# Two gate pairs a layer as plain filler units, a cover unit before the pairs, and the rotary tables built in the dense stage

## The chip, the core and the metric

The kernel runs on one core of a Trainium2 chip. The metric is the device time in microseconds (us) of one execution. Of the core's engines this text calls TensorE PE, VectorE DVE, ScalarE ACT, GpSimd POOL, and SyncE, which issues most of the DMA transfers, SP.

## What is computed

Two layers of a decoder trunk, 1024 tokens by 1024 channels in float32. From the normed input one product with `w_in` gives all that the three token mixers need, and the gates `g`:

```python
for l in range(DEPTH):
    h = rms_norm(x, norm_pre[l])
    u = h @ w_in[l]
    (a_q, a_k, a_v, a_z, b_q, b_kv, b_kr, b_z,
     c_q, c_k, c_v, c_z, g) = jnp.split(u, split_points, axis=-1)
    ...
    oa = diff_attention(..., lam, rel_bias)
    ob = mla_attention(q_nope, q_rope, k_nope, k_rope, v_m)
    oc = sliding_window_attention(..., sw_sinks[l], rel_bias)
    gates = jax.nn.sigmoid(g).reshape(B, S, N_BRANCHES, D_MODEL)
    y = (gates[:, :, 0] * ((oa * jax.nn.silu(a_z)) @ w_br_a[l])
         + gates[:, :, 1] * ((ob * jax.nn.silu(b_z)) @ w_br_b[l])
         + gates[:, :, 2] * ((oc * jax.nn.silu(c_z)) @ w_br_c[l]))
    x = x + rms_norm(y @ w_out[l], norm_post[l])
    x = x + jax.nn.sigmoid(x @ w_ple_gate[l]) * (p[l] @ w_ple_proj[l])
```

`lam` comes from four learned vectors a layer; the rotary part of the latent attention (MLA) needs the cosine and sine of position times frequency. The 3072 gate columns are 24 tiles of 128, eight for each branch, and are wanted only in the merge.

## The kernel before

**Products.** A float32 operand is split into a high and a low part, and a product is three matmuls (`group`, L296): high by high, high by low, low by high. A *unit* is one tile of 128 columns of `w_in` times the whole normed input: two halves of 512 tokens, eight blocks of 128 channels, three matmuls each, so 48 matmuls. It is a generator that yields after every six matmuls, and its weights come by `load_w` (L280): a DMA into one of two raw buffers (`wr`), a cast on ACT for the high part (L78), a subtraction on DVE or POOL (L93) for the low one; `le` says which. The matmuls of units carry the line L305, the split has L78 and L93 wherever it is used.

**A layer** runs these stages in order: an entry; `seven`, the dense stage; the sliding-window mixer `sw` (branch c); the differential mixer `da` (branch a); the latent entry `mla_entry` and the latent mixer `mla` (branch b); `merge`; and the tail with the output and embedding products.

**The dense stage** starts with the four z units of branch a, while DVE forms tiles `T`, sums and differences of blocks of the input. Then come *pairs*: `pair` makes two tiles of 128 columns with seven products in place of eight (Strassen's scheme over 2 x 2 blocks). Each product is 12 matmuls (L544), a pair 84. Its weights are two raw tiles, its combinations of weights `S` (L529), `aH` and `aL`; the sums of products `po` are made on DVE (L568, L583 and after). Four pairs are the z tiles of branches b and c (with silu on POOL), four are the gate tiles of branch a.

**Fillers.** The 16 gate tiles of branches b and c are plain units (`g_unit`), queued in `later` and taken out by `fill` and `weave` six matmuls at a time between the steps of a mixer. While gate units head the queue, each step adds `RATE` of the running mixer to a credit, and a chunk is taken when the credit reaches 1. A unit that is not used up by the mixers runs in full ahead of the merge. Its evictions are copied by ACT to `zs` (L78) and stored by SP to `g_d`. The merge loads the gates back, and applies the sigmoid to those of branches b and c.

**What is built once.** `setup_vecs`, `setup_lambda` and `setup_trig` run in layer 0's `sw`, between the two key groups. `setup_lambda` loads `lm` for each layer into one buffer (L180), POOL multiplies (L185), DVE sums (L187), ACT takes the exponent (L188). `setup_trig` computes the angles by some 40 operations of 128 x 128 on DVE, two sines on ACT (L252, L255), transposes on PE (L263), and stores the tables to `rope_d` for the latent entry.

**The latent entry** loads 416 columns of `w_in` in four chunks through the raw buffers `wr` (L1053), splits them into `WH` and `WL`, and makes eight row groups of 24 matmuls (stationary the input, moving 416 columns). `da` ends with a norm: ones products (L840), a square root on ACT (L896), reciprocal and product on DVE (L898); its result is transposed on PE (L639), which the program asks for behind the first row group.

**The order.** A scheduler places the instructions of each engine by priority and by what it believes to be ready; split and evictions are marked urgent (`high_priority`). Each engine then runs its own list in order. So where a filler stands is settled before the run.

Of the kernel before, what the change touches and what calls it, by code (L numbers as in the profile page):

```python
# [10 lines left out]
F32 = mybir.dt.float32  # L11
# [6 lines left out]
P = 128  # L18
S = 1024
D = 1024  # L20
DEPTH = 2
KT = D // P
# [6 lines left out]

RATE = dict(c=1.0, a=0.35, b=0.35)  # L30
BANKS = dict(mm=2, av=1, sc=3, tr=2)
# [29 lines left out]
class Builder:  # L61
# [44 lines left out]
    def setup(self):  # L106
# [3 lines left out]
        self.big = self.pool("big")  # L110
        self.w = self.pool("w")
        self.ent = ExitStack()
        pe = self.pool("entry", self.ent)
# [100 lines left out]

    def setup_trig(self, tp):
        nc, pi = self.nc, self.pi
        ang, v, k, d1, d0, a1 = (tp.tile([P, P], F32, name=n) for n in
                                 ("ang", "vv", "kk", "d1", "d0", "a1"))
        V = nc.vector
# [29 lines left out]
        V.tensor_scalar(ang, ang, PI_BELOW, -PI_BELOW, ALU.min, ALU.max)  # L249
        tr = tp.tile([P, 3, P], F32, name="trig")  # L250
        sn = tp.tile([P, 2, P], F32, name="sincos")
        nc.scalar.activation(sn[:, 0], ang, AF.Sin)  # L252
# [3 lines left out]
        V.tensor_scalar(tr[:, 0], sn[:, 0], -MLA_SCALE, None, ALU.mult)  # L256
        V.tensor_scalar(tr[:, 1:3], sn, MLA_SCALE, None, ALU.mult)

        self.cosT = self.cp.tile([P, 8, 2, 16], F32, name="cosT")
# [185 lines left out]

    def g_unit(self, l, bi, j):
        W = self.load_w(self.win(l, OFF["g"] + bi * D + j * P), le="g")

        def evac(hf, ps):
            st = self.zp.tile([P, 512], F32, tag="zs", bufs=2, name=self.uid("zs"))  # L450
            self.copy("a", st, ps)
            r0 = bi * D + j * P
            self.nc.sync.dma_start(self.g_d[r0:r0 + P, hf * 512:(hf + 1) * 512], st)

        yield from self.unit(W, KT, self.hT, evac)

    def seven(self, l):
        nc = self.nc  # L460
        with ExitStack() as ctx:
            z = [self.z_unit(l, "a", j) for j in range(4)]
            self.by_halves(*z[0:2])
            self.drain(*z[2:4])
            pl = self.pool("seven", ctx)
# [37 lines left out]
            for b in "bc":  # L503
                for j in (0, 2):
                    self.drain(self.pair(l, pl, T, OFF[b + "z"] + j * P, self.z_d[l, b], j * P, True))
            for j in range(0, KT, 2):
                self.drain(self.pair(l, pl, T, OFF["g"] + j * P, self.g_d, j * P, False))
# [149 lines left out]
    def sw(self, l):  # L657
        nc = self.nc
        with ExitStack() as ctx:
            pl = self.pool("sw", ctx)  # L660
# [26 lines left out]
            for g in range(2):  # L687
                if g == 1:
                    self.drain(*rest)
                    if not l:  # L690
                        self.setup_vecs()
                        self.setup_lambda(pl)
                        self.setup_trig(pl)
                for i in range(8):
# [348 lines left out]
    def mla_entry(self, l, p2, kH, kL, cq, ckv):  # L1043
# [13 lines left out]
        for hf in range(2):  # L1057
            raws = []
            st = p2.tile([P, 2, 4], F32, tag="st", bufs=2, name=self.uid("st"))
            for t in range(4):  # L1060
# [3 lines left out]
                                      lambda kt: tuple(x[:, sl] for x in self.hT[hf][kt]),  # L1064
                                      lambda kt: (WH[:, kt], WL[:, kt])), 1, not hf and t < 2)
                if self.rows_due:
# [67 lines left out]
    def merge(self, l):  # L1134
        nc, io = self.nc, self.io
        with ExitStack() as ctx:
# [50 lines left out]
            for bi, b in enumerate("abc"):  # L1187
                if b == "c":
                    self.yT = self.big_tiles()
                for j in range(KT):  # L1190
                    r0 = bi * D + j * P
                    s = pl.tile([P, S], F32, tag="sig", bufs=4, name=self.uid("sig"))
                    nc.sync.dma_start(s, self.g_d[r0:r0 + P, :])
                    if bi:
                        nc.scalar.activation(s, s, AF.Sigmoid)
# [160 lines left out]
    def build(self):  # L1356
# [3 lines left out]
        with self.ent:  # L1360
            self.entry()
            self.setup_bias(self.pe)
        self.zp = self.pool("zst")
        for l in range(DEPTH):
            self.seven(l)
            self.units = self.later(*[self.g_unit(l, bi, j) for bi in (1, 2) for j in range(KT)])
            for b, mixer in (("c", self.sw), ("a", self.da), ("b", self.mla)):
                self.rate = RATE[b]
                mixer(l)
            self.merge(l)  # L1370
            self.tail(l)
# [24 lines left out]
```

## Time and profile before

| | us |
|---|---|
| three runs | 2654.86 to 2656.57, median 2655.8 |
| the profiled execution | 2653.98 |
| its span in the trace | 2652.2 |

| engine | busy us | share of the span |
|---|---|---|
| PE | 2587.8 | 98% |
| DVE | 1659.6 | 63% |
| ACT | 1265.6 | 48% |
| POOL | 452.6 | 17% |

The busy time of PE counts matmuls; weight loads run beside them and are listed as PEld. A busy time is a sum over stages. Stages of the profiled execution, from the timeline (layer 0 and layer 1): z units 33 to 71 and 1342 to 1384; pairs to 229 and 1548; sliding window from 275 to 400 and from 1595 to 1700; differential mixer from 435 to 657 and from 1735 to 1974; latent entry to 738 and 2052; latent mixer to 937 and 2253; left-over gate units to 991 and 2305; then merge and tail. In a row of the timeline the figure in brackets is the engine's idle time ahead of the instruction, and behind the arrow stands what ended it.

### The profile page before, as it was taken

To read this page: it belongs to the slowest core of one execution; us is meant where nothing else is said; L and a number is where in the kernel's file an instruction comes from. 1 tells how busy PE (TensorE), PEld (TensorE's weight loads), DVE (VectorE), ACT (ScalarE), POOL (GpSimd) and SP (SyncE) were. 2 spreads that over 40 slices of the span, in tenths; PEclk is the share of its full clock that TensorE was granted. 3 is DMA by queue.
4 is the path that set the end of the run, shared out by engine and by line. 5 is a ranking of instruction groups with operands and counts; after the bars stand their busy time and mean duration, and the time that the engine had idled before them with its cause. 6 is when DMAs were issued, how large, how long until landed. Compare 5 with 4: busy or idle time off the path is not lost. (4 is left out here: it accounts for less than half of the span.)

```text
span 2652.2 us, 35930 instructions
## 1 busy us (share of the span) xinstructions
PE 2587.8 (98%) x12832; PEld 2120.4 (80%) x12832; DVE 1659.6 (63%) x3312; ACT 1265.6 (48%) x2761; POOL 452.6 (17%) x375
## 2 busy tenths in 40 slices
PE   8999999999999999999999999999999999999999
PEld 6778777888878878888877887888878788888887
DVE  7654565777378756755475536457764787577553
ACT  5433654555377733433443436545553777234332
POOL 2210000000010114234412001000000111251441
PEclk9999999999999999999999999999999999999999
DMA  6233123111110169453332331322111101894442
GB/s 197 86 116 109 46 69 104 53 52 48 51 31 23 53 210 290 148 177 115 116 96 90 114 99 50 94 68 60 51 53 40 29 22 54 267 280 148 137 118 96
DMA packets 296818, 269.21 MB, mean 102 GB/s; under 512 B 24272, under 2 KB 237456, under 8 KB 296512
## 3 DMA queue, kind: packets, MB, share of 16 engines
q1 hardware_dynamic: 295568, 262.19, 33.1%
q0 software_dynamic: 1072, 4.73, 0.6%
q8 instruction: 101, 1.65, 0.3%
q14 instruction: 77, 0.63, 0.1%
HBM read 194.93 MB, written 61.44 MB: 97 GB/s over the span
## 5 line engine op out<-in xcount | busy, mean ns | idle before, releaser
L305 PE MATMUL mm<-big,wH 128*128 128x512 f32 x3456 | 1106.5, 395 | 4.9 <-ACT zs L78 2.4
L305 PEld LDWEIGHTS mm<-big,wH 128*128 128x128 f32 x3456 | 638.9, 188 | 128.7 <-ACT zs L78 3.2
L305 PE MATMUL mm<-big,wL 128*128 128x512 f32 x1728 | 680.0, 394 | 2.3 <-POOL wL L93 1.9
L305 PEld LDWEIGHTS mm<-big,wL 128*128 128x128 f32 x1728 | 324.9, 188 | 65.7 <-POOL wL L93 2.8
L78 ACT CAST wH<-wr 128x1024 fp32r<-128x1024 f32 (+3 forms) x252 | 212.2, 852 | 334.4 <-PE mm L305 230.4
L93 DVE TENSOR_TENSOR wL<-wr,wH 128x1024 fp32r<-128x1024 f32 (+2 forms) x220 | 222.6, 1021 | 234.4 <-ACT wH L78 229.8
L793 ACT ACTIVATE e<-sc,st 128x512 f32<-128x512 f32 (+3 forms) x384 | 221.7, 582 | 99.5 <-DVE st L790 71.7
L787 DVE TENSOR_REDUCE st<-sc 128x1 f32<-128x512 f32 (+3 forms) x384 | 209.1, 551 | 7.2 <-PE sc L104 3.4
L93 POOL TENSOR_TENSOR wL<-wr,wH 128x1024 fp32r<-128x1024 f32 x32 | 77.4, 2423 | 501.7 <-ACT wH L78 336.6
L78 ACT CAST wtH<-tr 128x512 fp32r<-128x512 f32 x204 | 115.4, 590 | 82.5 <-PE tr L822 65.4
L93 DVE TENSOR_TENSOR wtL<-tr,wtH 128x512 fp32r<-128x512 f32 x204 | 136.3, 682 | 27.4 <-ACT wtH L78 26.9
L822 PE MATMUL tr<-cm,e 128*128 128x128 f32 x864 | 148.4, 275 | 1.0 <-DVE e L933 0.5
L544 PE MATMUL mm<-T,aH 128*128 128x512 f32 x384 | 121.5, 397 | 4.6 <-DVE po L583 3.9
L822 PEld LDWEIGHTS tr<-cm,e 128*128 128x128 f32 x864 | 106.1, 141 | 20.3 <-ACT e L793 7.0
L104 PE MATMUL sc<-kA,q 128*128 128x256 f32 (+3 forms) x320 | 104.6, 337 | 1.6 <-ACT e L735 0.8
L104 PE MATMUL sc<-kB,q 128*128 128x256 f32 (+3 forms) x320 | 99.6, 320 | 0.0
L544 PEld LDWEIGHTS mm<-T,aH 128*128 128x128 f32 x384 | 70.6, 188 | 26.3 <-DVE po L583 9.8
L544 PE MATMUL mm<-big,wH 128*128 128x512 f32 x256 | 82.9, 397 | 8.4 <-ACT po L78 8.4
L93 POOL TENSOR_TENSOR kL<-vT,kH 64x512 fp32r<-64x512 f32 x32 | 42.2, 1318 | 265.6 <-ACT kH L78 200.2
L379 POOL TENSOR_TENSOR acc<-acc,sq 128x512 f32<-128x512 f32 x36 | 56.8, 1577 | 176.2 <-ACT sq L378 176.2
L913 DVE TENSOR_TENSOR sc<-sc,dab 128x256 f32<-128x256 f32 (+1 forms) x128 | 52.4, 412 | 47.8 <-PE sc L104 46.6
L305 PE MATMUL mm<-WH,big 128*128 128x416 f32 x256 | 76.9, 370 | 3.6 <-ACT WH L78 2.7
(340 smaller groups left out, 5065.3 us busy)
## 6 DMA issues: line engine op xcount, KB each, us to landing
wr<-w_in SPq DMA_DIRECT2D x108, 512.0 KB, 3.8
sig<-g_d SPq DMA_DIRECT2D x48, 512.0 KB, 6.0
g_d<-zs SPq DMA_DIRECT2D x64, 256.0 KB, 2.2
wr<-w_out SPq DMA_DIRECT2D x32, 512.0 KB, 4.1
wr<-w_ple_gate SPq DMA_DIRECT2D x32, 512.0 KB, 4.0
kB<-kA SPq DMA_DIRECT2D x80, 128.0 KB, 2.3
x<-x SPq DMA_DIRECT2D x16, 512.0 KB, 6.1
g_d<-sg SPq DMA_DIRECT2D x32, 256.0 KB, 2.1
```

The lines of the kernel that those rows point to most:

```text
L78: nc.scalar.copy(out, in_)
L93: (nc.vector if le == "v" else nc.gpsimd).tensor_tensor(L, src, h, ALU.subtract)
L104: self.nc.tensor.matmul(ps, w, x, start=i == 0, stop=i == n - 1)
L305: self.nc.tensor.matmul(ps, w, x, start=i == 0, stop=i == n - 1)
L379: (nc.gpsimd if eng == "g" else nc.vector).tensor_tensor(st, st, sq, ALU.add)
L544: nc.tensor.matmul(ps, w, x, start=start and not i, stop=i == 11, skip_group_check=True)
L787: nc.vector.tensor_reduce(st[:, c:c + 1], ps[:, :w], AX.X, ALU.max, negate=len(ch) == 1)
L793: nc.scalar.activation(e[:, k0:k0 + w], pss[c][:, :w], AF.Exp, bias=st[:, 0:1], accum_out=sums[:, c:c + 1])
L822: self.nc.tensor.transpose(tr[:, (2 * a + q) * P:(2 * a + q + 1) * P], ws[q][:, kt * P:(kt + 1) * P], self.ident)
L913: nc.vector.tensor_tensor(ps[:, a - k0:w], ps[:, a - k0:w], bias[:, h, a - n + 256:k0 + w - n + 256], ALU.add)
```

## The change

- `PAIRED = 4`: only gate tiles 0 to 3 are still made by pairs (two pairs a layer). Tiles 4 to 7, which also belonged to pairs, join the units: 20 units a layer in place of 16. The merge applies the sigmoid to all tiles from 4 on.
- `RATE` rises from 0.35 to 0.4 in the differential mixer and to 0.45 in the latent one.
- In the latent entry all eight row groups are woven with a filler chunk after each six matmuls, at no credit; before, the first two of the first half were, and the others by credit.
- One unit, gate tile 23, is taken out of the queue and runs in the dense stage right behind the z units (the cover unit).
- `setup_trig` moves to the dense stage: its first part runs behind the pairs of branch b, its transposes and stores behind those of branch c. It works in three of the slots of the `T` tiles. `setup_vecs` and `setup_lambda` stay where they were.

```diff
-RATE = dict(c=1.0, a=0.35, b=0.35)
+RATE = dict(c=1.0, a=0.4, b=0.45)
+
+PAIRED = 4
...
-    def setup_trig(self, tp):
+    def setup_trig(self, room):
...
-        ang, v, k, d1, d0, a1 = (tp.tile([P, P], F32, name=n) for n in
-                                 ("ang", "vv", "kk", "d1", "d0", "a1"))
+        ang, v, k, d1, d0, a1 = (room[i // 4][:, i % 4 * P:i % 4 * P + P] for i in range(6))
...
         V.tensor_scalar(tr[:, 1:3], sn, MLA_SCALE, None, ALU.mult)
+        yield
...
-    def g_unit(self, l, bi, j):
-        W = self.load_w(self.win(l, OFF["g"] + bi * D + j * P), le="g")
+    def g_unit(self, l, n, le="g"):
+        bi, j = n // KT, n % KT
+        W = self.load_w(self.win(l, OFF["g"] + n * P), le=le)
...
             self.by_halves(*z[0:2])
-            self.drain(*z[2:4])
+            self.drain(*z[2:4], self.g_unit(l, 3 * KT - 1, le="v"))
...
-            for j in range(0, KT, 2):
+                if not l:
+                    if b == "b":
+
+                        trig = self.setup_trig([slot() for _ in range(3)])
+                    next(trig, None)
+            for j in range(0, PAIRED, 2):
                 self.drain(self.pair(l, pl, T, OFF["g"] + j * P, self.g_d, j * P, False))
...
                         self.setup_lambda(pl)
-                        self.setup_trig(pl)
...
-                                      lambda kt: (WH[:, kt], WL[:, kt])), 1, not hf and t < 2)
+                                      lambda kt: (WH[:, kt], WL[:, kt])), 1, True)
...
-                    if bi:
+                    if bi * KT + j >= PAIRED:
                         nc.scalar.activation(s, s, AF.Sigmoid)
...
-            self.units = self.later(*[self.g_unit(l, bi, j) for bi in (1, 2) for j in range(KT)])
+            self.units = self.later(*[self.g_unit(l, n) for n in range(PAIRED, 3 * KT - 1)])
```

How this moves instructions is shown at three places of PE's list. `mm` and `sc` are accumulators, `big` the parts of the normed input, `wH` and `wL` the split weights of a unit or of a pair's first tile. The lines of the changed kernel are a few higher (L305 is L309, L544 is L554, L639 is L649, L840 is L849).

Layer 0, PE, the end of the z units, before: the pair's first product follows the last z unit.

```order
L305 MATMUL mm_594<-big_164,wL_562 128x512
L305 MATMUL mm_594<-big_166,wH_561 128x512
L305 MATMUL mm_594<-big_167,wH_561 128x512
L305 MATMUL mm_594<-big_166,wL_562 128x512
L544 MATMUL mm_766<-big_136,wH_754 128x512
L544 MATMUL mm_766<-big_137,wH_754 128x512
```

The same place after: the last rows of the cover unit, which began 48 rows earlier, behind the last z unit.

```order
L309 MATMUL mm_657<-big_165,wL_626 128x512
L309 MATMUL mm_657<-big_167,wH_625 128x512
L309 MATMUL mm_657<-big_168,wH_625 128x512
L309 MATMUL mm_657<-big_167,wL_626 128x512
L309 MATMUL mm_657<-big_169,wH_625 128x512
L309 MATMUL mm_657<-big_170,wH_625 128x512
L309 MATMUL mm_657<-big_169,wL_626 128x512
L554 MATMUL mm_828<-big_139,wH_816 128x512
```

So 48 matmuls of a unit now stand between z units and pairs, in both layers.

Layer 0, PE, from the end of the differential mixer into the latent entry, before. `ms` is that mixer's norm, `WH` and `WL` the entry's weights; the six unit rows are the last of 17 behind the ones products.

```order
L305 MATMUL mm_6228<-big_164,wH_6175 128x512
L305 MATMUL mm_6228<-big_165,wH_6175 128x512
L305 MATMUL mm_6228<-big_164,wL_6176 128x512
L305 MATMUL mm_6228<-big_166,wH_6175 128x512
L305 MATMUL mm_6228<-big_167,wH_6175 128x512
L305 MATMUL mm_6228<-big_166,wL_6176 128x512
L639 MATMUL tr_6329<-cm,ms_3526 32x128
L305 MATMUL mm_6283<-WH_6264,big_136 128x416
L305 MATMUL mm_6283<-WL_6265,big_136 128x416
```

The same place after:

```order
L815 MATMUL av_5874<-wd_3283,VH_4908 128x256
L815 MATMUL av_5874<-wd_3282,VL_4909 128x256
L849 MATMUL av_5990<-ones,sq_5987 128x1 x2
L649 MATMUL tr_6125<-cm,ms_3291 32x128
L309 MATMUL mm_6069<-WH_6050,big_139 128x416
L309 MATMUL mm_6069<-WL_6051,big_139 128x416
L309 MATMUL mm_6069<-WH_6050,big_140 128x416
L309 MATMUL mm_6069<-WH_6050,big_141 128x416
```

No unit matmul is left between the ones products and the transpose of `ms`; the next one comes behind all 24 matmuls of the first row group.

Layer 1, PE, the same seam, before:

```order
L305 MATMUL mm_18387<-big_11772,wH_18334 128x512
L305 MATMUL mm_18387<-big_11771,wL_18335 128x512
L840 MATMUL av_18362<-ones,sq_18359 128x1 x2
L639 MATMUL tr_18488<-cm,ms_15685 32x128
L305 MATMUL mm_18442<-WH_18423,big_11741 128x416
L305 MATMUL mm_18503<-WH_18423,big_11741 128x416
```

And after, the end of the eleven unit rows that stand there now:

```order
L309 MATMUL mm_18146<-big_11709,wH_18142 128x512
L309 MATMUL mm_18146<-big_11708,wL_18143 128x512
L309 MATMUL mm_18146<-big_11710,wH_18142 128x512
L309 MATMUL mm_18146<-big_11711,wH_18142 128x512
L309 MATMUL mm_18146<-big_11710,wL_18143 128x512
L649 MATMUL tr_18247<-cm,ms_15410 32x128
L309 MATMUL mm_18201<-WH_18182,big_11696 128x416
```

In layer 1 the unit moved the other way: into the gap between the ones products and the transpose.

Over the whole program the unit matmuls of a layer go from 768 to 960. By stage, before and after, layer 0: dense stage 0 and 48, sliding window 192 and 158, differential mixer 192 and 226, latent entry 54 and 150, latent mixer 140 and 160, ahead of the merge 190 and 218. Layer 1: 0 and 48, 158 and 158, 226 and 250, 60 and 132, 134 and 163, 190 and 209.

## Rows read from the trace of the kernel before

**Rows 1.** The page's first part: busy us, share, instructions of each engine.

```profile
PE 2587.8 (98%) x12832; PEld 2120.4 (80%) x12832; DVE 1659.6 (63%) x3312; ACT 1265.6 (48%) x2761; POOL 452.6 (17%) x375
```

**Rows 2.** Busy time by stage: stretch, length, engines, granted clock, DMA share, GB/s.

```profile
275.40:400.00 124.60, 117.98 (x607) 96.40 (x605) 79.77 (x274) 74.31 (x217) 11.00 (x8) 0.97 0.24 60
...
657.50:738.00 80.50, 76.60 (x386) 66.18 (x386) 35.50 (x91) 28.08 (x71) 6.47 (x8) 0.98 0.15 46
738.00:937.00 199.00, 194.77 (x1177) 159.10 (x1176) 155.00 (x373) 147.79 (x397) 28.20 (x19) 1.00 0.13 36
...
1595.00:1700.00 105.00, 103.14 (x551) 83.67 (x550) 69.98 (x226) 69.49 (x211) 9.66 (x5) 1.00 0.23 64
...
1974.50:2052.00 77.50, 71.24 (x353) 61.48 (x353) 32.97 (x86) 25.14 (x66) 5.66 (x3) 0.96 0.16 46
```

**Rows 3.** Timeline of PE in a dense stretch of layer 1: start, us, instruction.

```profile
1358.28 0.62 PE L305 MATMUL mm<-big,wH 128*128 128x512 f32 x2
1358.73 0.39 PE L305 MATMUL mm<-big,wL 128*128 128x512 f32 x1
```

**Rows 4.** Busy time in three stretches: PE, PEld, DVE, ACT, POOL, clock.

```profile
33.00:71.00 38.00, 37.24 (x163) 30.16 (x162) 35.96 (x56) 16.70 (x27) 0.00 (x0) 1.00 0.34 103
110.00:130.00 20.00, 19.68 (x86) 15.84 (x85) 11.40 (x16) 7.77 (x12) 5.71 (x5) 1.00 0.34 106
343.00:356.40 13.40, 9.25 (x38) 7.45 (x37) 11.26 (x44) 4.18 (x7) 2.46 (x1) 0.85 0.27 82
```

**Rows 5.** Timeline of PE at the start of layer 1's first pair.

```profile
1397.02 1.22 PE L544 MATMUL mm<-big,wH 128*128 128x512 f32 x2 [7.47 <-ACT po L78]
...
1400.49 0.39 PE L544 MATMUL mm<-big,wL 128*128 128x512 f32 x1
```

**Rows 6.** Waits of PE from 30 to 110 us: total us, times, longest.

```profile
PE mm L544 <- DVE po L583: 1.6, 2, 1.3
PE mm L544 <- ACT po L78: 1.0, 1, 1.0
```

**Rows 7.** Timeline of PE in layer 0's sliding window.

```profile
353.45 0.47 PE L263 MATMUL tr<-cm,sincos 128*128 128x128 f32 x1 [4.15 <-ACT sincos L252]
```

**Rows 8.** Timeline of SP and POOL in layer 0's sliding window: the lambda chain.

```profile
333.45 0.58 SPq L180 DMA_DIRECT2D lm<-da_lambda  x1
...
337.61 0.46 POOL L185 TENSOR_TENSOR pr<-lm 128x128 f32<-128x128 f32 x1 [3.90 <-DMA lm<-da_lambda]
...
341.59 0.46 POOL L185 TENSOR_TENSOR pr<-lm 128x128 f32<-128x128 f32 x1 [3.52 <-DMA lm<-da_lambda]
```

**Rows 9.** Timeline of PE from layer 1's norm into its latent entry.

```profile
1984.66 0.37 PE L639 MATMUL tr<-cm,ms 128*32 128x128 f32 x1 [2.21 <-DVE ms L898]
1985.70 1.03 PE L305 MATMUL mm<-WH,big 128*128 128x416 f32 x2 [0.67 <-ACT WH L78]
...
1990.64 0.45 PE L305 MATMUL mm<-WL,big 128*128 128x416 f32 x1
...
1999.67 0.50 PE L305 MATMUL mm<-big,wL 128*128 128x512 f32 x1 [0.95 <-POOL wL L93]
```

**Rows 10.** Timeline of ACT, SP and PE at the start of layer 0's latent entry.

```profile
664.67 0.37 ACT L78 COPY o<-av 128x256 f32<-128x256 f32 x1 [1.55 <-PE av L806]
...
667.76 1.68 ACT L78 CAST WH<-wr 128x832 fp32r<-128x832 f32 x2 [0.77 <-DVE ms L898]
...
672.04 0.91 SPq L1053 DMA_DIRECT2D wr<-w_in  x2
...
675.75 0.89 ACT L78 CAST WH<-wr 128x832 fp32r<-128x832 f32 x1 [5.12 <-DMA wr<-w_in]
...
676.68 1.06 PE L305 MATMUL mm<-WH,big 128*128 128x416 f32 x2 [2.01 <-ACT WH L78]
...
677.72 1.43 SPq L277 DMA_DIRECT2D wr<-w_in  x2
...
681.63 1.05 ACT L78 CAST wH<-wr 128x1024 fp32r<-128x1024 f32 x1 [3.94 <-DMA wr<-w_in]
...
685.18 0.50 PE L305 MATMUL mm<-big,wL 128*128 128x512 f32 x1 [0.94 <-POOL wL L93]
```

More of the change, by code (lines that the diff above doesn't have):

```diff
@@ L111, in setup @@
         self.w = self.pool("w")
+        self.zp = self.pool("zst")
         self.ent = ExitStack()
@@ L249, in setup_trig @@
         V.tensor_scalar(ang, ang, PI_BELOW, -PI_BELOW, ALU.min, ALU.max)
-        tr = tp.tile([P, 3, P], F32, name="trig")
-        sn = tp.tile([P, 2, P], F32, name="sincos")
+        tr = room[2][:, 0:3 * P].rearrange("p (a j) -> p a j", j=P)
+        sn = room[1][:, 2 * P:4 * P].rearrange("p (a j) -> p a j", j=P)
         nc.scalar.activation(sn[:, 0], ang, AF.Sin)
@@ L1362, in build @@
             self.setup_bias(self.pe)
-        self.zp = self.pool("zst")
         for l in range(DEPTH):
             self.seven(l)
-            self.units = self.later(*[self.g_unit(l, bi, j) for bi in (1, 2) for j in range(KT)])
+            self.units = self.later(*[self.g_unit(l, n) for n in range(PAIRED, 3 * KT - 1)])
             for b, mixer in (("c", self.sw), ("a", self.da), ("b", self.mla)):
```

## The prediction

> **What bounds the kernel now.** I read the busy shares first. TensorE (PE) is busy 2587.8 us of 2652.2 [rows 1], so the end moves only if PE gets fewer matmuls, shorter waits, or less time at the lower clock. The windows by stage say where the waits are [rows 2]: the sliding-window mixer of layer 0 idles 6.62 us of 124.6, its twin in layer 1 1.86 of 105.0; the latent entries idle 3.90 and 6.26 us; the granted clock is under 1.00 in all of these but the twin. Then the order of the changed kernel shows, on PE, what stands in each hole, and I go back to the timeline for what each hole costs. All is counted against the profiled execution (2653.98 us); the median of the three runs is 2655.8, 1.8 higher, and I add the difference to the median.
>
> **More matmuls: +10.8 us.** Where nothing waits, two matmuls of 512 columns take 0.45 us from start to start, 0.225 each [rows 3]. A pair makes two tiles with seven products of 12, 84 matmuls; two plain units take 96. Two pairs in each of two layers become units: 4 x 12 = 48 more, 48 x 0.225 = 10.8, all on PE. The order counts the same: 960 gate-unit matmuls a layer where 768 stood. The waits of pairs that the profile names lie in the first ones and in those with silu, so I let nothing come back with the gate pairs. The Trainium skill ("TensorE: Matmul & The Clock Gate", Back-to-back issue gap) has a sustained 131 ns for 512 columns; by it this term would be 6.3 us. The rows here say 225, and the measurement decides.
>
> **Cover unit: -11.9 us (-8 to -13).** Between the last z unit and the first pair now stand 48 matmuls of a gate unit, 10.8 us, which need only the normed input. What they cover is the wait for VectorE, which forms the T tiles and is busy 35.96 us of 38 there [rows 4]. In layer 1 PE idles 7.47 us before the pair's third product and then runs eight matmuls from 1397.02 to 1400.49 at the lower clock, 3.47 us in place of 1.80 [rows 5]; the starts on either side of the hole make it 7.6, so 9.3 in all. The hole is under 10.8, so the unit covers it whole. In layer 0 the waits before the pairs' products are 1.6 + 1.0 us by cause [rows 6]. The unit's own split adds one VectorE pass of 1.2 us, and if its weights come late the gain shrinks: the low end, -8. The 48 matmuls are no cost here: they left the mixers.
>
> **Tables out of the mixer, layer 0: -5.3 us (-7.5 to +1).** In the mixer PE waits 4.15 us for the sine [rows 7], and then runs at the lower clock until 359; the stage as a whole idles 4.8 us more than its twin and grants 0.97 against 1.00 [rows 2]. From 353.45 to 359 at half rate 2.8 us are lost: together 7.6. After the change PE's order there is that of layer 1 but for two exchanges. What stays is the lambda chain: two loads one behind the other on SP through one buffer, then a GpSimd product, then VectorE. GpSimd waited 3.90 and 3.52 us for its loads [rows 8] and VectorE for GpSimd, and nobody minded, since some hundred unit matmuls, 23 us, ran. Those matmuls are gone from there. From the first load's issue (333.45) to the second product's end (341.59 + 0.46) are 8.6 us [rows 8]. VectorE's score reductions and ScalarE's exponents are queued behind. Laid over layer 1's timeline, the products come about 1 us after each is wanted: 2.2 us, nearer to the small end of 0.5 to 8.6, because two score tiles are already through. -7.5 + 2.2 = -5.3 (at 8.6, +1).
>
> **The tables in the dense stage: +1.0 us (0 to +12).** VectorE's table work is 11.3 us of 13.4 in the old place [rows 4]. It now lies in two pairs of 20 us, each with 11.4 us of VectorE work [rows 4]: 17 of 20 us, no overflow. But the pairs wait for VectorE's sums, in order; one sum late by some short operations of 0.28 us gives about 1 us. Eight stores of the tables precede one weight load on SP, which is wanted a pair later. ScalarE reloads its function tables three times more, with 12 us of 20 free [rows 4]. If nothing overlaps, all of the 11.3 us shows: the high end.
>
> **Latent entry of layer 1: -6.2 us (-3 to -9).** Before, PE reaches the norm chain (square root, reciprocal, transpose) with no unit matmul left: 2.21 us, 0.67 for a weight cast, then a run at the lower clock to 1990.64, 14 matmuls of 416 columns 0.353 us apart in place of 0.183 (0.225 x 416/512): 2.4; and a wait of 0.95 for GpSimd's weight split [rows 9]. Sum 6.2. In the new order 11 unit matmuls (2.5 us) stand in the norm chain, and the second half of that unit, its weights long loaded, follows.
>
> **Latent entry of layer 0: +8 us (+4 to +13).** Here it is the reverse. Before, 17 unit matmuls cover the norm chain; PE idles 2.01 us for the third weight chunk, runs slowly to 680 (about 2.3 by the same count), and waits 0.94 for GpSimd's split [rows 10]: 5.3. After, the unit ends before the last weighted block, the transpose of the norm follows the ones product at once, and all 24 products of the first row group stand in a row. The next unit's weights come fifth through two raw buffers, behind four chunks. Its hole in steps, from rows of before [rows 10]: the norm chain from the last product's eviction (664.67) to the first cast (667.76) and its 0.9: 3.5 us idle. The third chunk may be issued when the first chunk's split on VectorE ends, about 669.7 (the third one's cast ends at 676.64 and the load behind its split goes at 677.72, so a split is 1.1), and lands 3.7 later as it does now (672.04 to 675.75), cast 0.9: 674.3; PE has done its 12 products at 671, idle 3.3. The unit's load goes after the third chunk's split, at 675.4, lands 3.9 later (677.72 to 681.63) and is cast in 1.05: 680.3, where PE was done at 676.7: 3.6. Then 1.5 for the GpSimd split (2.4 us less the work beside it), and 1.6 to 2.3 at the lower clock. Sum 13.5 to 14.2, less 5.3: 8.2 to 8.9; I take 8, since the last weighted block may slip into the first hole.
>
> **The rest of both entries: -1.7 us (-3 to 0).** Of the idle time [rows 2] 2.4 us in layer 1 and 0.95 in layer 0 are short waits that I haven't named. The change weaves a chunk of unit matmuls after each chunk of all eight row groups (before: the first two), 96 and 72 matmuls more: half of it may go.
>
> **Mixers at the higher rate: -2 us (-4 to +3).** Layer 0's latent mixer idles 4.2 us of 199 [rows 2], in many short waits. 20 more unit matmuls there, and 29 in layer 1, may take a quarter of it in each, a us apiece; if they push the softmax's products later, it costs as much. For the differential mixer I take nothing. The merge's four more sigmoids a layer lie on a ScalarE that is a third busy: nothing.
>
> **Sum.** 10.8 - 11.9 - 5.3 + 1.0 - 6.2 + 8 - 1.7 - 2 = -7.3. Profiled 2646.7; on the median 2648.5.
>
> **The rivals.**
> *Both entries run full (faster still).* If the scheduler's order matters less than I think and the weights of layer 0's unit arrive with the chunks, the +8 falls to 0 or below, as in layer 1: 2640.5, and with no cost of lambda 2638.3. For it: the split is marked urgent. Against it: two raw buffers and an in-order SP. Chance 0.15.
> *Lambda's chain takes the place of the sine (no change).* If the chain lies bare for its 8.6 us in place of 2.2, the mixer gives back 6.4: 2654.9. For it: the 7.4 us that its loads took. Against it: score tiles ahead of it. Chance 0.22. The same time comes out if the fillers' extra matmuls in the mixers find no hole and the cover gives only its low end (2 and 3.9 gone: 2654.4).
> *The dry entry of layer 0 (slower).* If after each of its three holes PE stays at the lower clock until 690, the 24 chunk products (4.5 us) and some 30 of the unit (6.8) cost twice their time: 11.3 us, less the 2 already counted, 9 more. The unit's load behind the norm's row store on SP could add 3 to 4 more, and one more run at the lower clock 2. It decides from 20.5 us in this stretch, for which all of it must come: 2661 and more, to 2664. For it: after the holes of [rows 5] and [rows 9] the clock was low for 3.5 and 5 us. Against it: three separate runs would need 20 us of low clock, and no row shows such a run. Chance 0.15. The Trainium skill (the same page, Part 1) calls half rate the resting state that activity lifts; that speaks for this rival, and the trace agrees as far as each of the long holes is followed by such a run.
> *It does not do what it says.* Cover and fillers stand in the order, so only their weights could fail; that is the low end above.
>
> **How the numbers follow.** My forecast has 0.48 with its own range 2643 to 2654, the rivals 0.15, 0.22 and 0.15. A measurement of this kernel can tell about 0.2%, 5.3 us. Of the forecast's 0.48 some 0.13 lie above 2650.5, so faster is 0.35 + 0.15 and a little of the second rival: 0.52; same 0.13 and most of the 0.22, less what of both ends over 2661: 0.31; slower 0.15 and that: 0.17. The range is 2638 to 2663: the better case's lower end and the slower case's upper one lie outside with some 0.08 each.
>
> **What would show it.** Right: no PE wait over 1 us before layer 1's first pairs; 48 matmuls of a unit ahead of them; layer 0's mixer without the sine's wait, with one of 1 to 3 us for lambda; 13 to 14 us lost between the last weighted block and the first unit in layer 0's entry, and nearly none in layer 1's. Wrong: pairs three and four of layer 0 longer than 20.5 us (tables), lambda's wait over 5 us, or layer 0's entry as full as layer 1's.

## The result, and the profile after

The changed kernel takes 2668.62 us (four runs, 2666.64 to 2673.01) against 2655.33 before (the median of four): a ratio of 1.0051, with an interval of 1.0036 to 1.0066. It is slower by 13.3 us, where 2648.5 was forecast, and it lies above the range, which ended at 2663.

The page's first part of the kernel after, to be read against [rows 1]:

```profile
PE 2602.3 (98%) x12880; PEld 2132.9 (80%) x12880; DVE 1615.2 (61%) x3254; ACT 1261.1 (47%) x2747; POOL 465.8 (17%) x381
```

48 matmuls more, as counted; 14.5 us more of busy PE, of which 10.8 are theirs. The span is 2667.3 us, 15.1 longer.

To find the place I cut both executions into stretches at the same instructions (first and last product of the pairs, transposes of the mixers, first step of the merge), and took from each stretch its matmuls at the pace of full speed: 0.227 us for 512 columns, in proportion for fewer. What is left is time lost to waits, to the lower clock and to switches between operations. Its change, after less before:

| stretch | layer 0 | layer 1 | forecast, both |
|---|---|---|---|
| 48 more matmuls | +5.4 | +5.4 | +10.8 |
| z units to the last pair | -4.3 | -10.2 | -10.9 |
| sliding window, to the differential mixer | -5.9 | +1.5 | -5.3 |
| differential mixer | +1.2 | +0.7 | 0 |
| latent entry, with what leads to the latent mixer | +7.4 | -4.6 | +0.1 |
| latent mixer | -1.9 | +3.1 | -2 |
| left-over units ahead of the merge | **+6.4** | **+7.0** | 0 |
| merge, then tail | 0 | +4.0 | 0 |

The gains are there, and larger than forecast where they were largest. The loss stands in a row that the sum did not have: the left-over units between the last product of the latent mixer and the merge, 13.4 us. Busy time by stage of the kernel after (columns as in [rows 2]):

```profile
250.00:348.00 98.00, 94.93 (x512) 76.99 (x510) 66.72 (x214) 65.31 (x199) 10.95 (x8) 1.00 0.25 60
632.00:722.00 90.00, 83.42 (x369) 70.43 (x368) 24.28 (x63) 22.97 (x56) 10.47 (x5) 0.92 0.20 58
...
936.00:998.30 62.30, 57.92 (x246) 46.65 (x245) 25.91 (x32) 16.83 (x27) 12.29 (x7) 0.95 0.78 247
...
1957.00:2036.00 79.00, 75.94 (x360) 66.02 (x359) 22.08 (x62) 21.60 (x55) 8.12 (x4) 0.98 0.20 60
...
2256.40:2316.00 59.60, 55.89 (x239) 45.46 (x238) 23.82 (x32) 16.34 (x26) 12.78 (x7) 0.94 0.77 248
```

The same view of the kernel before, for the two stretches ahead of the merges:

```profile
940.30:991.40 51.10, 49.92 (x225) 40.96 (x224) 26.74 (x32) 15.49 (x26) 9.93 (x5) 1.00 0.77 254
2256.50:2305.10 48.60, 48.58 (x221) 40.09 (x220) 26.02 (x32) 15.47 (x25) 10.39 (x5) 1.00 0.81 267
```

Before, PE idles 1.2 us and nothing there, at full clock; after, 4.4 and 3.7, with a granted clock of 0.95 and 0.94. The two longest waits of PE from 935 to 1000 us after name the operands (total us, times, longest):

```profile
PE mm L309 <- ACT wH L80: 2.1, 1, 2.1
PE mm L309 <- POOL wL L95: 1.7, 1, 1.7
```

`wH` and `wL` are the split weights of the last left-over unit. The timeline of POOL after shows when their raw buffer came free, with the split of the unit two places ahead:

```profile
945.18 2.39 POOL L95 TENSOR_TENSOR wL<-wr,wH 128x1024 fp32r<-128x1024 f32 x1 [19.18 <-ACT wH L80]
```

And the timeline of SP after shows when their load was issued, the first of two rows:

```profile
973.60 0.38 SPq L281 DMA_DIRECT2D wr<-w_in  x1
974.08 0.64 SPq L281 DMA_DIRECT2D wr<-w_br_a  x1
```

The buffer is free at 947.6; the load goes at 973.60, when the loads of ten of the merge's blocks (three or four each) and the gates' stores have passed SP in order. (In the kernel before, the last unit's load went at 944.11.) Behind the late load come the cast on ACT, 978.82, and the split on POOL, 2.35 us. PE waits for one and then the other, and goes on at the lower clock, as its timeline after shows:

```profile
979.92 0.73 PE L309 MATMUL mm<-big,wH 128*128 128x512 f32 x2 [2.09 <-ACT wH L80]
982.35 0.79 PE L309 MATMUL mm<-big,wL 128*128 128x512 f32 x1 [1.70 <-POOL wL L95]
...
983.79 0.63 PE L309 MATMUL mm<-big,wL 128*128 128x512 f32 x1
984.22 1.05 PE L309 MATMUL mm<-big,wH 128*128 128x512 f32 x2
```

From 983.79 to 984.22 one matmul takes 0.43 us in place of 0.227; the granted clock from 982 to 986 us is 0.50. The Trainium skill ("TensorE: Matmul & The Clock Gate", Part 1) gives 426.7 ns from start to start for 512 columns at the lower rate; the trace agrees with 0.43.

What had been forecast for the other places can be read in four short answers. The waits of PE from 1358 to 1420 us after (layer 1's first pairs; before, 7.47 us, [rows 5]):

```profile
PE mm L309 <- POOL big L95: 0.7, 2, 0.4
PE mm L309 <- DVE big L95: 0.3, 1, 0.3
PE mm L554 <- DVE po L593: 0.3, 1, 0.3
```

The cover holds. The waits of PE in layer 0's sliding window after (250 to 348; before, the sine, [rows 7]):

```profile
PE av L106 <- ACT wtH L80: 1.2, 2, 1.0
PE sc L106 <- ACT wtH L80: 1.1, 5, 0.4
```

The sine is gone; for lambda one wait of 1.0 us is left, at 306.7, just behind the chain's first exponent on ACT (305.96). The tables' price stands in the third silu pair of layer 0, which takes 21.7 us from its first product to the next pair's, where it took 19.8 before. PE's timeline there:

```profile
133.12 0.73 PE L554 MATMUL mm<-T,aH 128*128 128x512 f32 x2 [2.17 <-DVE po L593]
```

DVE's timeline just ahead of it, three table operations in a row and then the sum that PE waits for:

```profile
131.53 0.93 DVE L231 SCALAR_TENSOR_TENSOR T<-T 128x128 f32<-128x128 f32 x3
132.38 0.68 DVE L593 TENSOR_TENSOR po<-mm,po 128x512 f32<-128x512 f32 x1
```

And the dry start of layer 0's latent entry, PE after (before: [rows 10]):

```profile
635.53 0.27 PE L649 MATMUL tr<-cm,ms 128*32 128x128 f32 x1 [1.76 <-DVE ms L907]
636.56 0.69 PE L309 MATMUL mm<-WH,big 128*128 128x416 f32 x1 [0.77 <-ACT WH L80]
...
638.04 0.89 PE L309 MATMUL mm<-WH,big 128*128 128x416 f32 x2
638.74 0.55 PE L309 MATMUL mm<-WL,big 128*128 128x416 f32 x1
...
647.84 0.73 PE L309 MATMUL mm<-big,wH 128*128 128x512 f32 x2 [0.93 <-ACT wH L80]
...
650.28 0.79 PE L309 MATMUL mm<-big,wL 128*128 128x512 f32 x1 [1.03 <-POOL wL L95]
```

From 638.04 to 638.74 two matmuls of 416 columns take 0.35 us each in place of 0.18; the granted clock from 636.5 to 646 us is 0.50. From the last weighted block (632.13) to 653.5, where the full pace is back, 14.4 us are lost: PE idles 5.9 of them, and the other 8.5 are matmuls at the slower pace and the restarts behind each wait.

The third chunk and then the unit are loaded as worked out, counted from the last weighted block; SP's timeline after:

```profile
637.50 1.33 SPq L1062 DMA_DIRECT2D wr<-w_in  x2
...
642.79 10.20 SPq L281 DMA_DIRECT2D wr<-w_in  x4
```

And ACT's timeline after, with the casts that PE waits for:

```profile
640.82 0.89 ACT L80 CAST WH<-wr 128x832 fp32r<-128x832 f32 x1 [3.62 <-DMA wr<-w_in]
...
646.74 1.05 ACT L80 CAST wH<-wr 128x1024 fp32r<-128x1024 f32 x1 [3.81 <-DMA wr<-w_in]
```

### The profile page after: what moved, and what is told of

Same layout as the page of the kernel before. It is cut to its first block, busy times and chain, and to the rows that moved or that the text cites. A ratio compares the mean times of both kernels' runs of the same rounds, so it can differ in the third digit from the quotient of the medians.

```text
span 2667.3 us, 35903 instructions
## 1 busy us (share of the span) xinstructions
PE 2602.3 (98%) x12880; PEld 2132.9 (80%) x12880; DVE 1615.2 (61%) x3254; ACT 1261.1 (47%) x2747; POOL 465.8 (17%) x381
## 4 chain that ended last, share of the span: by engine, by line
PE 70%; DVE 5%; DMA 4%; ACT 4%; issue 3%; POOL 1%; SPq 0%; ACTq 0%; DVEq 0%; POOLq 0%
PE mm L309 42%; PE sc L106 8%; PE av L815 5%; PE sc L309 4%; PE tr L831 3%; PE mm L554 2%; DMA wr<-w_in 2%; PE tr L309 1%; DMA sig<-g_d 1%; ACT wH L80 1%; PE sc L554 1%; DVE wL L95 1%; ACT e L744 0%; PE av L849 0%; PE tr L1024 0%
## 5 line engine op out<-in xcount | busy, mean ns | idle before, releaser
L309 PE MATMUL mm<-big,wH 128*128 128x512 f32 x3712 | 1190.8, 396 | 12.9 <-ACT wH L80 5.0
L309 PEld LDWEIGHTS mm<-big,wH 128*128 128x128 f32 x3712 | 688.6, 189 | 148.4 <-ACT wH L80 6.3
L309 PE MATMUL mm<-big,wL 128*128 128x512 f32 x1856 | 734.4, 396 | 6.4 <-POOL wL L95 5.5
L309 PEld LDWEIGHTS mm<-big,wL 128*128 128x128 f32 x1856 | 350.8, 189 | 78.6 <-POOL wL L95 8.0
L95 POOL TENSOR_TENSOR wL<-wr,wH 128x1024 fp32r<-128x1024 f32 x38 | 91.0, 2396 | 628.0 <-ACT wH L80 548.5
L554 PE MATMUL mm<-T,aH 128*128 128x512 f32 x288 | 90.5, 396 | 4.3 <-DVE po L593 4.3
L309 PE MATMUL mm<-WH,big 128*128 128x416 f32 x256 | 82.1, 375 | 3.3 <-ACT WH L80 2.1
L567 POOL TENSOR_TENSOR sg<-po,sg 128x512 f32<-128x512 f32 x32 | 45.1, 1411 | 218.0 <-ACT sg L565 169.7
L802 ACT ACTIVATION_READ_ACCUMULATOR e<-sc,st 128x1 f32 x384 | 76.5, 199 | 0.0
```

The costliest lines, as they stand in the source:

```text
L95: (nc.vector if le == "v" else nc.gpsimd).tensor_tensor(L, src, h, ALU.subtract)
L309: self.nc.tensor.matmul(ps, w, x, start=i == 0, stop=i == n - 1)
L554: nc.tensor.matmul(ps, w, x, start=start and not i, stop=i == 11, skip_group_check=True)
L567: nc.gpsimd.tensor_tensor(sg, src, sg, ALU.mult)
L802: nc.scalar.activation(e[:, k0:k0 + w], pss[c][:, :w], AF.Exp, bias=st[:, 0:1], accum_out=sums[:, c:c + 1])
```

## The experiments

The theory after the result: two loads of unit weights come late, that of the last left-over unit ahead of each merge (13 us, and what was thought to follow from it, the 4.0 in layer 1's tail) and that of the first unit in layer 0's entry (9 us); all else does about what was forecast. The main rivals: the stretch ahead of the merge is short of DMA anyway (its share is 0.78 there), so that no order of the loads helps; or the higher rates cost the mixers.

| run | what differs | us | ratio to before |
|---|---|---|---|
| e1 | changed, unit loads urgent | 2655.66 | 1.0002 (0.9993 to 1.0012) |
| e2 | changed, rate 0.42 in the differential mixer | 2654.18 | 0.9997 (0.9987 to 1.0006) |
| e3 | changed, cover unit behind the pairs | 2683.46 | 1.0110 (1.0095 to 1.0125) |
| e4 | changed, all four gate pairs | 2700.26 | 1.0169 (1.0154 to 1.0184) |
| e5 | changed, rates 0.42 and 0.55, urgent | 2653.27 | 0.9991 (0.9982 to 1.0001) |
| e6 | changed, rates 0.42 and 0.35, urgent | 2648.30 | 0.9974 (0.9964 to 0.9983) |
| e7 | changed, tables back in the mixer | 2674.25 | 1.0069 (1.0053 to 1.0086) |
| e8 | three gate pairs, rates 0.42 and 0.30, urgent, half of the entry woven by credit | 2652.38 | 0.9983 (0.9973 to 0.9992) |
| e9 | before, latent mixer's rate 0.30 | 2684.60 | 1.0113 (1.0096 to 1.0130) |
| e10 | four gate pairs, rates 0.375 and 0.20, urgent, entry woven as before | 2666.15 | 1.0046 (1.0031 to 1.0061) |
| e11 | three gate pairs, rates 0.375 and 0.30, urgent, entry woven as before | 2672.31 | 1.0067 (1.0052 to 1.0082) |
| e12 | changed, six chunks at the seam | 2648.33 | 0.9978 (0.9969 to 0.9987) |
| e13 | changed, six chunks at the seam, urgent | 2640.04 | 0.9946 (0.9933 to 0.9958) |

**The late load ahead of the merge.** Undone (e1):

```diff
-        W = self.load_w(self.win(l, OFF["g"] + n * P), le=le)
+        with self.tc.high_priority():
+            W = self.load_w(self.win(l, OFF["g"] + n * P), le=le)
```

> The changed kernel, with the weight loads of gate units marked urgent for the scheduler; nothing else. On SP the load of the fifth left-over unit then stands 30 rows ahead of the first branch weights where it stood 1 ahead, behind 3 of the merge's loads in place of 10. Theory (the late load): the 6.4 and 7.0 us lost ahead of the two merges go, about 2668.6 - 13 = 2655, and no wait of PE over 0.5 us stands there. Rival (the stretch is short of DMA: its share is 0.77 there): the load lands as late, the loss stays within 3 us and the time at 2665 to 2669. Rival (more fillers in the latent mixer cost the time): no change, 2668.

2655.66: 13.0 us back. The last load of a unit in layer 0, on SP's timeline in e1:

```profile
949.28 0.38 SPq L281 DMA_DIRECT2D wr<-w_in  x1
```

And the busy time of e1 ahead of layer 0's merge:

```profile
937.50:992.30 54.80, 54.80 (x248) 45.15 (x247) 28.13 (x32) 16.79 (x27) 12.35 (x7) 1.00 0.84 269
```

The load goes 24 us earlier than at 973.60, PE has no idle time at all, and the DMA share is higher than in the changed kernel, 0.84: it was the load's place in SP's list, not a shortage. PE has as many matmuls in each stretch as in the changed kernel. In the layer-by-layer count the two stretches lose 7.9 and 4.8 us less; in layer 1 two waits for evictions (`zs`), 1.5 us together, are left there. Layer 1's merge and tail, which had lost 4.0, lose 3.8 less, but that hole does not hang on the late load: in e12 the load in layer 1 stays late (7.2 us lost against before) and the tail loses only 0.3, in e11 the load is early and the tail loses 4.2. In the changed kernel it is PE's waits at the first output products for the merge's result, 1.6 us the longest; what makes them come and go is open.

Brought about in the kernel before, by one number that has nothing to do with the change (e9):

```diff
-RATE = dict(c=1.0, a=0.35, b=0.35)
+RATE = dict(c=1.0, a=0.35, b=0.3)
```

> The kernel before with one number changed: the latent mixer's rate 0.30 in place of 0.35. Ten matmuls of units more are left ahead of each merge (201 and 199 in place of 190), and with that the last unit's load moves on SP from 40 rows ahead of the first branch weights to 1 ahead, behind 10 of the merge's loads. Nothing else of the change is in it. Theory (the late load by itself costs 6 to 7 us a merge): 2655 + 12 = 2664 to 2670. Rival (the loss needs the changed kernel's units, its cover or its entry): 2654 to 2657.

2684.60, 30 us slower, where 2664 to 2670 was expected. Ten left-over matmuls more move the last load from 944.11 to 980.02 on SP; the largest wait of PE ahead of layer 0's merge in e9:

```profile
PE mm L305 <- ACT wH L78: 5.4, 1, 5.4
```

And ahead of layer 1's:

```profile
PE mm L305 <- ACT wH L78: 7.5, 1, 7.5
```

With the lower clock behind them these stretches lose 6.3 and 11.6 us more than before: the mechanism needs neither cover nor entry nor units in place of pairs. Most of the other 12 us of e9 lie in the latent mixers (+4.5 and +5.4); ten matmuls fewer are not worth that by their number, so this is the order of that kernel, which I haven't followed further.

**The seam ahead of the latent entry.** First by the differential mixer's rate (e2):

```diff
-RATE = dict(c=1.0, a=0.4, b=0.45)
+RATE = dict(c=1.0, a=0.42, b=0.45)
```

> The changed kernel with the differential mixer's rate 0.42 in place of 0.40. The order then has 12 and 14 unit matmuls between the ones products and the transpose in layers 0 and 1, where the changed kernel has 0 and 11, and the next ones four rows after. The number of unit matmuls in the mixer itself grows by less than 20. Theory (the seam of layer 0 is dry by the phase at which a unit ends): the stretch from the last weighted block to the end of the entry's row groups in layer 0 loses 9 us less, layer 1's stays; time 2668.6 - 9 = 2659 to 2660. Rival (a higher rate costs the mixers): the differential mixer grows by over 2 us and the gain is under 5. The last load ahead of the merge stays late, so its 13 us stay by the theory of the late load.

2654.18, 14.4 less, more than the seam could give. The start of layer 0's entry lost 10.2 us less, but 5.3 came back in the steps before the latent mixer, and layer 1's latent mixer lost 5.3 less. The last load ahead of the merges stays late here, as expected, and so do its losses (6.4 and 5.8 us against before). The rate moved too much at once. So the seam alone (e12):

```diff
-FILL = (3, 2, 2, 1, 1, 5, 4)
+FILL = (3, 2, 2, 1, 1, 5, 6)
```

> The changed kernel with one number changed: behind the differential mixer the program takes six filler chunks in place of four. Each layer then has 11 unit matmuls between the ones products and the transpose, and the next unit's weights are asked for ahead of the entry's chunks. Theory (layer 0's entry is dry because its unit ends ahead of the chunks, so that the next unit's load waits behind them): the stretch from the last weighted block to the entry's last row group loses 8 to 10 us less in layer 0 and about 2 in layer 1, the rest stays: 2668.6 - 10 = 2658 to 2660. Rival (the gain of the run with rate 0.42 came from the mixers, not from the seam): under 4 us.

Busy time in e12 of the entry of layer 0 and of the steps behind it:

```profile
632.50:710.60 78.10, 75.39 (x364) 65.30 (x363) 24.41 (x62) 21.11 (x55) 8.14 (x4) 1.00 0.22 66
710.60:734.80 24.20, 22.12 (x100) 16.33 (x99) 15.92 (x36) 14.01 (x33) 5.77 (x8) 0.93 0.11 33
```

The entry loses 10.5 us less, at full clock; 4.5 come back behind it, where PE idles 2.1 us and the clock drops. That the next unit's weights have to be asked for ahead of the chunks is shown. But the run is 20.3 us faster, and the seam's net is 6: the rest is small, in ten stretches, the largest again layer 1's latent mixer with 5.0 and layer 1's tail with 3.8, neither of which the theory had (2658 to 2660 was expected). The order of the units behind the seam changes with it, as in e2, and I can't say why it frees layer 1's latent mixer; what goes there is mostly waits for split weights (PE idles 5.2 us in that mixer in the changed kernel, 1.4 in e12). In e10 and e11 (rate 0.375) the seam is dry again, with 11.5 and 9.0 us lost in layer 0 against before and 5.7 and 4.7 in layer 1, although seven unit matmuls stand in the norm chain there. Their next unit is again loaded behind the chunks, which agrees; but these two also differ in pairs and weaving.

**Both repairs** (e13):

> Both repairs and nothing else: six chunks at the seam and urgent weight loads, at the changed rates 0.40 and 0.45. Theory (the two losses are separate and make up the whole miss): 2668.6 - 13 - 10 = 2645 to 2647, which is the blind forecast less the seam. Rival (they overlap): 2650 or more.

2640.04 us, below both kernels: 0.54% under before, 8 under the forecast, and 5 under what was expected of this run. More came back than the two losses, because layer 1's latent mixer (5.2 us) and tail (3.0) go with the seam's change. The late load and the seam of layer 0 with the steps behind it give 10.2 and 7.0. The page's first part of e13:

```profile
PE 2590.3 (98%) x12880; PEld 2125.6 (81%) x12880; DVE 1620.8 (61%) x3254; ACT 1260.1 (48%) x2747; POOL 464.5 (18%) x381
```

And its busy time ahead of the two merges:

```profile
928.20:983.90 55.70, 53.09 (x237) 43.06 (x237) 27.21 (x32) 16.31 (x26) 11.90 (x6) 1.00 0.75 250
...
2235.20:2288.70 53.50, 52.58 (x237) 43.10 (x236) 28.79 (x32) 16.26 (x26) 11.49 (x6) 1.00 0.80 259
```

The clock is full in both; the 2.6 and 0.9 us that PE idles there are waits for evictions.

**Cover and tables.** The cover moved behind the pairs (e3), and the tables moved back (e7):

```diff
-            self.drain(*z[2:4], self.g_unit(l, 3 * KT - 1, le="v"))
+            self.drain(*z[2:4])
...
+            self.drain(self.g_unit(l, 3 * KT - 1, le="v"))
```

> The changed kernel with the cover unit run at the end of the dense stage, behind the last pair, in place of ahead of the first. Theory (the cover hides DVE's forming of the T tiles): the waits of before come back at the first pairs, 3 us in layer 0 and 9 to 10 in layer 1: 2668.6 + 12.5 = 2681. Rival (the first pairs no longer wait because the tables left or the pairs are fewer): within 3 us of 2668.6.

```diff
...
-                if not l:
-                    if b == "b":
-
-                        trig = self.setup_trig([slot() for _ in range(3)])
-                    next(trig, None)
...
+                        self.setup_trig(pl)
```

> The changed kernel with the rotary tables back in layer 0's sliding-window mixer, the rest as changed. Theory: the wait for the sine and the run at the lower clock come back, 7 us, the wait of the lambda chain (1.1 us) hides behind it again, and the dense stage gets back the 2.3 us before the fourth silu pair's sum: 2668.6 + 7 - 1 - 2 = 2672 to 2673. Rival (the tables cost the dense stage as much as they cost the mixer): within 1.5 us of 2668.6.

2683.46, so the cover is worth 14.8 us here (expected 12.5), and 2674.25, so moving the tables is worth 5.6 (expected 3.4 to 4.4). The waits of PE in e3 at layer 0's pairs:

```profile
PE mm L555 <- ACT po L80: 4.5, 1, 4.5
PE mm L555 <- DVE po L594: 2.8, 3, 2.2
```

At layer 1's first pairs in e3:

```profile
PE mm L555 <- ACT po L80: 7.4, 1, 7.4
```

And the largest in e7's sliding window of layer 0:

```profile
PE tr L266 <- ACT sincos L255: 4.6, 1, 4.6
```

Layer 1's hole comes back as it was; layer 0's is 4.5 us there where it was 1.0 before [rows 6], so the cover gives more in layer 0 than the kernel before could show.

**What the pairs are worth, and the rates.** All gate pairs back (e4):

```diff
-PAIRED = 4
+PAIRED = 8
```

> The changed kernel with all four gate pairs a layer again (PAIRED 8), the rest as changed: 48 matmuls of 512 columns fewer, and about 20 unit matmuls left ahead of the merge in place of 210 to 218. Theory: 10.9 us of work and the 13.4 us of the late load go, layer 0's dry seam stays (its order is the same): 2668.6 - 24 = 2644 to 2645. Rival (the work of two pairs costs no more than its pairs' waits, and the merge's start is bound by its own loads): the merge then waits for its gated tiles, and the time is 2655 to 2660, with PE waits over 5 us ahead of the merge.

2700.26, where 2644 was expected: the theory missed by 56 us. Some 20 unit matmuls are left ahead of each merge, and the merge's start has nothing to run beside its loads. PE's waits in e4 from 978 to 1146 us:

```profile
PE tr L309 <- ACT wH L80: 6.9, 1, 6.9
PE mm L309 <- ACT oH L80: 5.3, 3, 3.6
```

The stretch ahead of the merge and the merge lose 18.6 us more than the changed kernel in layer 0 and some 22 to 24 in layer 1, by where the merge's end is cut. So the left-over units are not work that happens to be late: they are the cover of the merge's first loads. e10 keeps all pairs and 178 left over, by lower rates and the entry woven as before:

> All four gate pairs a layer, with the cover unit and the tables in the dense stage, rates 0.375 and 0.20, the latent entry woven as before, urgent loads; 178 unit matmuls are left ahead of each merge, where the run with all pairs at the changed rates had 20. Theory (that run's 30 us were a merge that starts with nothing to run beside its loads, and the pairs' work is worth 10.8 us): the start of the merge loses under 4 us a layer and the time is 2648 - 10 + 4 = 2640 to 2645. Rival (fewer fillers in the latent mixer cost what the pairs save): the latent mixers lose 5 us or more beyond before and the time is 2648 or more.

2666.15, above its range, with the merges as forecast (within 0.3 us of before, and 0.7 and 3.3 more just ahead of them), but with the dry seams named above and 3.6 and 4.8 us in the latent mixers. Three pairs were tried twice, e8 and e11:

> Three gate pairs a layer (PAIRED 6), rates 0.42 and 0.30, urgent weight loads, and the latent entry woven at no credit in its first half only, so that 199 and 195 unit matmuls are left ahead of the merges. 24 matmuls fewer than in the run with 0.42 and 0.55. Theory (a pair saves 12 matmuls of 0.225 us a layer and fillers are worth nothing beyond covering the seams and the start of the merge): 5.4 us below that run, 2636 to 2638. Rival (the fillers that are missing in the latent mixer cost as much as the pair saves): 2641 to 2645.

> Three gate pairs a layer, rates 0.375 and 0.30, the latent entry woven as before, urgent loads; 243 and 227 unit matmuls left ahead of the merges. Theory: 24 matmuls fewer than in the run with 0.42 and 0.35, -5.4 us, and the starts of the merges as in that run: 2643 to 2645. Rival (as with the other six-paired kernel, a slip of the order in layer 1's latent mixer and merge takes it back): 2648 to 2652.

2652.38 and 2672.31, where 2636 to 2638 and 2643 to 2645 were expected: in both the saved 5.4 us of work are gone. e8 lost them in layer 1's latent mixer (8.5 more than in e2) and merge (7.2), e11 at its seams and in both latent mixers (5.4 and 4.3 more than before). Whether a kernel with more pairs can be the fastest is left open.

The rate of the latent mixer, 0.55 (e5) and 0.35 (e6) at otherwise equal settings:

> The changed kernel with the differential mixer's rate 0.42, the latent mixer's rate 0.55 and urgent weight loads of gate units. 186 unit matmuls are then left ahead of each merge (190 in the kernel before), and both seams have unit matmuls between ones products and transpose. Theory (the late load and the dry seam are the two losses, and they are separate): both go, 2668.6 - 13 - 14 = 2641 to 2643, faster than before by 0.4 to 0.5%. Rival (the losses overlap, or a rate of 0.55 costs the latent mixer's softmax its turn): the latent mixers grow by more than their extra matmuls and the time is 2647 or more.

> As the run before, but with the latent mixer's old rate 0.35; 220 and 227 unit matmuls are left ahead of the merges. It measures the higher rate by itself. Theory (the prediction's term: 40 more unit matmuls a layer fill a quarter of the mixer's waits): 2 to 4 us slower than at 0.55. Rival (the mixer's waits are switches that no filler takes away): within 1.5 us of it. Rival (the higher rate delays the softmax): faster than at 0.55 by 2 us or more.

2653.27 and 2648.30. The higher rate is slower by 5 us, as the third theory of e6 had it, but not by delaying the softmax: the latent mixers lose 2.6 us less at 0.55 in layer 0 and 0.2 more in layer 1. It is the merges that lose: their starts 0.8 and 3.0 and the merges 1.0 and 2.9 us more, with 186 unit matmuls left in place of 220 and 227; that the smaller number is the cause is not shown. The two repairs did not add up in e5 (2641 to 2643 was expected), nor fully in e13: one by one they gave 13.0 (e1) and 20.3 us (e12), together 28.6.

## Why the prediction was wrong

- **More matmuls, +10.8:** right. 48 more, and the changed kernel's sum of matmuls at full pace is 10.8 larger.
- **Cover, -11.9, and tables in the dense stage, +1.0:** right in sign, too small by 3.6 together; -14.5 measured in the dense stages. The tables cost 2.2 us at one sum of pair three, where one late sum was priced at 1, and that pair's 21.7 us are over the 20.5 that the text had named as a sign of being wrong; the cover gave more.
- **Tables out of the mixer, -5.3:** right (-5.9). Lambda's wait is 1.0 us; the rival that made it 8.6 fell.
- **Latent entries, +8 and -6.2 and -1.7:** right in both signs; +7.4 and -4.6. That layer 0's 14.4 us lie beside the 13.5 to 14.2 of the text is luck in its make-up. The loads came as worked out, but PE was taken to run at full pace between them: its waits were to be 3.5, 3.3, 3.6 and 1.5, 11.9 us, with 1.6 to 2.3 at the lower clock. Measured are 5.9 idle (norm chain 0.75 + 1.76 + 0.77, third chunk at most 0.34, unit 0.93, POOL 1.03) and 8.5 at the lower clock: PE ran the first row group at half pace and so was still busy when the third chunk came. The slower rival, which had the clock low behind each hole, was right in that, but the full pace was back at 653.5, some 4 us earlier than it had it, and its price did not come. Layer 1 gained less than forecast; PE still waits 1.35 us for a chunk's cast and 0.79 for a unit's there.
- **Mixers, -2:** wrong in layer 1, +3.1 in place of -1, about 2 of it in more waits for split weights. Why they come is not explained; they go in e2, e5, e6, e12 and e13, which all have another seam.
- **The step that failed is a term that is not in the sum: the left-over units were put at nothing.** The text counts 20 and 29 more unit matmuls in the mixers, and the counts by stage ahead of it show 218 and 209 left ahead of the merges where there were 190. I took left-over units as work merely moved, at no price, and did not ask where the loads of one more unit would stand on SP, nor did any rival. A fifth unit had to be loaded, ten blocks of the merge's loads came ahead of it, and 13.4 us were lost there; e1 and e9 show that the place of that load does it. This alone turns -7.3 into +6.1. The 9 that are missing to 15.1 are layer 1's tail (4.0, cause open), the latent mixers (3.2), the entries (2.7) and the other mixers (2.8), less 3.6 that cover and tables gave beyond their terms.

The list of SP in both kernels would have shown it: the last load of `w_in` stands 40 rows ahead of the first branch weights before, 1 row ahead after.

## What to carry to other kernels

Work that is moved is free only if its inputs move with it: for each unit that changes its place, find its load on the in-order queue, what stands ahead of it and when its buffer came free. In this kernel filler work has two ends that matter more than its rate: the seams between stages, where the next unit must have been asked for before the stage's own loads, and what is left over at the end, which here covers the next stage's first loads, is too little at 20, and at 200 and more has its last load too late unless that load is asked for early. A change that gains at the places it was made for can lose it all at one place that the diff does not touch.

## What the runs showed that was not expected

One number in a filler's rate (0.35 to 0.30 in e9) costs the tuned kernel 30 us, of which 18 lie ahead of the merges, because ten matmuls more carry the last unit's load behind the merge's. And the some 190 unit matmuls ahead of each merge that look like a remainder are worth over 30 us: with 20 left in place of 210 the kernel (e4) needs 2700.26 us, 31.6 more than the changed one, although it has 48 matmuls less to do.
